# One more gate product by seven, three heads at a time, and weight sums over whole groups, in a gated hybrid transformer block

## The chip, the cores and the metric

One core of one Trainium2 chip runs the kernel in a single launch. Its engines are TensorE (PE, with the weight loads as PEld), VectorE (DVE), ScalarE (ACT), GpSimd (POOL) and SyncE (SP), which issues almost all transfers. The metric is the device time of one execution in microseconds (us), and the median over several executions where there are several. All inputs and the output are float32 in device memory.

## The reference, cut to what matters

One transformer block over 256 tokens of width 2048 (`q`, `k`, `v` heads of 128 columns):

```
h    = rms_norm(x)                                    # 256 x 2048
proj = h @ w_in                                       # 2048 x 11270: q,k,v of 6 + 6 heads, logits, 4 memory heads, 3 gates x 2048
o_fox = softmax(q k^T scale + c_q - c_k, causal) @ v  # 6 heads; c: running sums of log_sigmoid(logits)
log_beta = log_sigmoid(z);  z = q k^T scale           # 6 stick-breaking heads
log_1m   = where(before, log_beta - z, 0)
a        = where(before, exp(log_beta + sum of log_1m over later keys), 0);  o_sb = a @ v
o_mem = softmax(q mk^T scale) @ mv                    # 4 heads; mk, mv = rms_norm(mem) @ w_mem_kv
g     = sigmoid(gates + b_gate)                       # three gates of 256 x 2048
merged = g0*(o_fox @ w_br_fox) + g1*(o_sb @ w_br_sb) + g2*(o_mem @ w_br_mem)
x = x + merged @ w_out                                # 2048 x 2048
u = conv3(rms_norm(x) @ w_up)                         # 2048 x 11264
out = x + (silu(u[:, :5632]) * u[:, 5632:]) @ w_down  # 5632 x 2048
```

## The kernel before

**Three passes.** A weight tile of 128 x 1024 is loaded by SP (`raw`, L140), ACT rounds it to the matmul type (`hi`, L141), DVE subtracts to get the rest (`lo`, L142), and each product is three matmuls: rows of x high with `hi`, low with `hi`, high with `lo` (`passes` L148, `three` L284). `product` (L156) runs a whole product of 256 rows and n columns over pairs of k-tiles, one raw tile per pair, and calls `tick` after each pair. Rings of four tiles each (`WBUFS`, `SBUFS`) hold raw, hi and lo.

**Blocks by eight and by seven.** `blocked` (L324) computes 1024 columns at a time over pairs of k-tiles. A pair has two blocks of rows, two of k and two of columns, so plainly it has 8 block products of three matmuls each (`eight`, L346). A pair "by seven" has 7 products of sums of blocks instead, as in Strassen's scheme in Winograd's form. It needs sums of x (`pair_sums`, L290: five DVE sums, copies on ACT and subtractions) and sums of the weight blocks. After the last seven of a block, four banks `Y` are added into the four results (`gather`, or `gathered` at L963 for the gates). The order of a block's pairs is a string, `e` for an eight, `s` for a seven, `f` for forming the sums of x of one pair (L225 to L227):

```
o_plans = ("eessesse", "eesesese")
g_plans = (("", "", "esesesee"), ("esesesee", "esesesee", "esesesee"))
d_plans = ("ef" * 5 + "ssef" * 4 + "seeee", "efefefesssfe" + "ssse" * 2 + "ssssee")
```

`g_plans[m][b]` is for gate b in columns m x 1024 on, and an empty string means two plain products of 512 columns.

**Where weight sums come from.** For the gates `prepared` (L393, four DVE sums) makes them on the spot, one entry of the plan ahead (`ahead`). For the output product (o) and the down projection (d), they are made long before: `weight_sums` (L243) takes halves of groups of 256 of 512 columns from a queue `halves`, loads the half into a staging tile, makes the sums with three DVE additions (L267 to L269) and stores them in device memory (`kept`, L272). It is a generator that `tick` moves on by one step. `seven` (L369) later loads two raw tiles, two sums T1 and T2, and T3, T4 from there.

**The order of work.** `tick` (L102) moves every generator of `background` on, and up to `WINDOW` = 2 of the queue that `later` fills: heads (`mem_head`, `fox_head`, `sb_head`), transposes (`heads_T`, `merged_T`), gathering. A generator `yield`s where others' work comes between. A stick-breaking head (L871) makes z on PE, log_beta and log_1m on ACT and DVE, two selects on POOL (`diagonal`, L863), splits into `ls` (L890, L891), sums with PE into r (L895), then DVE, ACT's exp, two more selects, and the product with v (`weighted`). `in_order` keeps an instruction at its program place on its engine; the rest is put in order by the scheduler. SP issues its transfers strictly in one order, so a load behind a store waits for that store's data.

**The stages.** kv of the memory, the memory queries (`mq`), the forgetting heads' products f0 to f4 (the last with 262 columns, L780), the stick-breaking ones s0 to s4 (s4 with 256, L913), gates for columns 0 to 1023 (m = 0) with the heads beside them, branches, gates m = 1, branches, output product o (two blocks), up projection (L1159, with convolution and silu beside it), and down projection d (two blocks of 22 pairs, L1225). The sums of x for the gates, `xs` (L840), lie in the slot of the residual `xres`, which is loaded a second time at L1017. Sums of a pair for d lie in `sf` (L1198) or, in the second block, where the pairs of x no longer needed were.

## Time and profile before

| what | value |
| --- | --- |
| runs (three), median | 1467.25 us (1466.77 to 1467.32) |
| profiled execution, its own time | 1466.63 us |
| its span | 1464.9 us |
| PE busy | 1459.6 us, 7335 records |
| PEld / DVE / ACT / POOL busy | 1235.3 / 1192.2 / 839.0 / 21.7 us |
| transfers | 369.55 MB, mean 252 GB/s |
| granted clock, whole span | 1.000 |

A page of the profile is one execution. Busy time sums the time in which an engine had an instruction at work, in us and as a share of the span; matmuls overlap each other, so the mean of one matmul in the groups (394 ns) is more than its share of the time. Names are the program's, and L12 is line 12 of the code above. In a group, `out<-in` names the tiles, x counts instructions, and after the bar stand busy us, the mean ns of one, and idle time ahead with what ended it. A row of waits reads: engine, tile and line that waited, what released it, us in sum, count, longest. A tile name is the program's: `lo_s` belongs to the products s0 to s4, `pre_d` is a staging tile of the weight sums for d.

### The profile page before, as it was taken

The page shows a single profiled execution, that of the slowest core. Times are in us where ns is not written, and L with a number is a line of the kernel's source. Part 1 is how long each engine was busy: PE and PEld are TensorE (multiplying, and loading weights), DVE is VectorE, ACT ScalarE, POOL GpSimd, SP SyncE. Part 2 cuts the span into 40 slices and gives each one's busy share as a digit, 9 for nine tenths or more (in the row PEclk, how much of TensorE's full clock was granted, in tenths as well). Part 3 has the DMA queues.
Part 4 walks back from the last instruction along what each step waited for, and adds up shares of the span by engine and source line. Part 5 has one row for each costly group of instructions (what it writes and reads, how often), then busy time and mean ns, then how long its engine had stood idle before and what let it go on. Part 6 is the DMA issues. An engine that isn't in the chain of part 4 may idle for free.

```text
span 1464.9 us, 20666 instructions
## 1 busy us (share of the span) xinstructions
PE 1459.6 (100%) x7335; PEld 1235.3 (84%) x7335; DVE 1192.2 (81%) x1816; ACT 839.0 (57%) x1194; POOL 21.7 (1%) x48
## 2 busy tenths in 40 slices
PE   9999999999999999999999999999999999999998
PEld 7888888888888888888888888888888888888887
DVE  5777676776588899997877889888888887997887
ACT  6755454464364455546666656556556556674664
POOL 0000000021000000000000000000000000000000
PEclk9999999999999999999999999999999999999999
DMA  9686787687868576778777889888888876798796
GB/s 309 198 281 189 222 279 218 186 265 217 258 190 281 169 222 203 270 260 279 257 194 229 276 281 294 276 282 289 288 285 284 277 235 196 254 319 267 263 333 215
DMA packets 205606, 369.55 MB, mean 252 GB/s; under 512 B 13578, under 2 KB 82078, under 8 KB 205246
## 3 DMA queue, kind: packets, MB, share of 16 engines
q1 hardware_dynamic: 204094, 365.99, 78.3%
q10 hardware_dynamic: 1328, 2.11, 0.4%
q8 instruction: 57, 0.93, 0.2%
q14 instruction: 47, 0.39, 0.1%
q0 software_dynamic: 80, 0.13, 0.0%
HBM read 335.67 MB, written 32.51 MB: 251 GB/s over the span
## 4 chain that ended last, share of the span: by engine, by line
PE 99%; DVE 0%; ACT 0%; POOL 0%; issue 0%; POOLq 0%; DVEq 0%
PE u L1174 22%; PE u L1175 11%; PE xd L288 4%; PE xd L287 4%; PE xd L286 4%; PE xg L286 3%; PE xg L287 3%; PE xg L288 3%; PE f L288 2%; PE f L286 2%; PE f L287 2%; PE s L286 2%; PE s L288 2%; PE s L287 2%; PE g L286 2%; PE b L286 2%
## 5 line engine op out<-in xcount | busy, mean ns | idle before, releaser
L1174 PE MATMUL u<-hT,hi_u 128*128 128x512 f32 x1232 | 428.3, 394 | 0.0
L1175 PE MATMUL u<-hT,lo_u 128*128 128x256 f32 x1232 | 341.4, 277 | 0.0
L1174 PEld LDWEIGHTS u<-hT,hi_u 128*128 128x128 f32 x1232 | 231.0, 188 | 53.6
L142 DVE TENSOR_TENSOR lo_u<-raw_u,hi_u 128x1024 fp32r<-128x1024 f32 x176 | 214.9, 1221 | 63.8 <-ACT hi_u L141 62.9
L141 ACT CAST hi_u<-raw_u 128x1024 fp32r<-128x1024 f32 x176 | 184.8, 1051 | 137.1 <-PE u L1174 120.5
L1175 PEld LDWEIGHTS u<-hT,lo_u 128*128 128x128 f32 x1232 | 231.3, 188 | 0.0
L281 DVE TENSOR_TENSOR lo_d<-raw_d,hi_d 128x1024 fp32r<-128x1024 f32 x88 | 106.8, 1223 | 20.2 <-ACT hi_d L280 17.5
L280 ACT CAST hi_d<-raw_d 128x1024 fp32r<-128x1024 f32 x88 | 91.8, 1053 | 47.6 <-PE xd L287 22.2
L280 ACT CAST hi_g<-raw_g 128x1024 fp32r<-128x1024 f32 (+1 forms) x64 | 61.7, 972 | 37.7 <-PE xg L287 12.4
L281 DVE TENSOR_TENSOR lo_g<-raw_g,hi_g 128x1024 fp32r<-128x1024 f32 (+1 forms) x64 | 70.9, 1117 | 4.3 <-ACT hi_g L280 4.3
L141 ACT CAST hi_f<-raw_f 128x1024 fp32r<-128x1024 f32 (+1 forms) x40 | 38.5, 966 | 52.1 <-PE f L287 47.3
L142 DVE TENSOR_TENSOR lo_f<-raw_f,hi_f 128x1024 fp32r<-128x1024 f32 (+1 forms) x40 | 44.7, 1119 | 27.9 <-ACT hi_f L141 25.9
L287 PE MATMUL xd<-hi_d,aT 128*128 128x512 f32 x170 | 66.2, 389 | 0.0
L286 PE MATMUL xd<-hi_d,aT 128*128 128x512 f32 x170 | 66.2, 389 | 0.0
L288 PE MATMUL xd<-lo_d,aT 128*128 128x512 f32 x170 | 66.2, 389 | 0.0
L142 DVE TENSOR_TENSOR lo_s<-raw_s,hi_s 128x1024 fp32r<-128x1024 f32 (+1 forms) x40 | 44.7, 1117 | 25.2 <-ACT hi_s L141 24.6
L141 ACT CAST hi_s<-raw_s 128x1024 fp32r<-128x1024 f32 (+1 forms) x40 | 38.4, 961 | 43.9 <-PE s L287 27.1
L1174 PE MATMUL u<-hT_rest,hi_u 128*128 128x512 f32 x176 | 62.0, 394 | 0.0
L1125 ACT ACTIVATE y<-u,taps 128x256 f32<-128x256 f32 x88 | 49.6, 596 | 17.0 <-DVE u L1120 16.9
L142 DVE TENSOR_TENSOR lo_g<-raw_g,hi_g 128x1024 fp32r<-128x1024 f32 x32 | 39.3, 1232 | 22.9 <-ACT hi_g L141 22.4
L141 ACT CAST hi_b<-raw_b 128x1024 fp32r<-128x1024 f32 x32 | 33.5, 1052 | 40.5 <-PE b L287 13.5
L141 ACT CAST hi_g<-raw_g 128x1024 fp32r<-128x1024 f32 x32 | 33.6, 1050 | 37.7 <-PE g L287 34.8
(482 smaller groups left out, 3533.7 us busy)
## 6 DMA issues: line engine op xcount, KB each, us to landing
raw_u<-in_w_up_dram SPq DMA_DIRECT2D x176, 512.0 KB, 5.1
raw_g<-in_w_in_dram SPq DMA_DIRECT2D x96, 512.0 KB, 4.3
raw_d<-in_w_down_dram SPq DMA_DIRECT2D x66, 512.0 KB, 5.1
pre_d<-in_w_down_dram SPq DMA_DIRECT2D x88, 256.0 KB, 4.5
kept_d<-pre_d SPq DMA_DIRECT2D x44, 512.0 KB, 6.1
raw_f<-in_w_in_dram SPq DMA_DIRECT2D x32, 512.0 KB, 4.7
raw_s<-in_w_in_dram SPq DMA_DIRECT2D x32, 512.0 KB, 3.8
raw_o<-in_w_out_dram SPq DMA_DIRECT2D x25, 512.0 KB, 5.5
```

Of the source, the lines that this page charges most:

```text
L141: pin(nc.scalar.copy(hi[:, :m], raw[:, :m]))
L142: pin(nc.vector.tensor_tensor(lo[:, :m], raw[:, :m], hi[:, :m].bitcast(F32), ALU.subtract))
L280: nc.scalar.copy(hi[:, :n], src)
L281: nc.vector.tensor_tensor(lo[:, :n], src, hi[:, :n].bitcast(F32), ALU.subtract)
L286: fix(nc.tensor.matmul(o, lhsT=ah, rhs=w[0], start=first, stop=False))
L287: fix(nc.tensor.matmul(o, lhsT=al, rhs=w[0], start=False, stop=False))
L288: fix(nc.tensor.matmul(o, lhsT=ah, rhs=w[1], start=False, stop=last))
L1125: nc.scalar.activation(y, u[:, 2:], AF.Identity, scale=tap(2), bias=tap(3))
L1174: nc.tensor.matmul(ps[i], lhsT=hi[:, j, c], rhs=hT(k + j), start=first, stop=False)
L1175: nc.tensor.matmul(ps[i][:, :S], lhsT=lo[:, j, c], rhs=hT(k + j)[:, :S], start=False, stop=last)
```

## The change

Plans: the second gate of the first 1024 columns gets the string of the others; the second output block has four sevens instead of three; the two blocks of d have 11 and 14 sevens instead of 9 and 13. That is 33 groups with kept sums for o and d instead of 29, and five of the six gate blocks by seven instead of four.

Weight sums: `pair_sums_ahead` takes whole groups (one load of 128 x 2048, three additions, one store), one per six steps during the products f0 to s3, in two staging tiles in the slot of `xres`, the sums three steps and the store five steps after the load. `half_sums` goes on with halves during the gates. In the up projection there is one stream of whole groups in one staging tile `ends`, from step 22 on, one per eight steps.

Heads: the window is three from the queueing of the stick-breaking heads until the first block by seven asks for their end, and two elsewhere. The sums of x for the gates move from the queue into the background of the first gate's product, with junk tiles for scratch.

Down projection: eleven pairs' sums are formed in the first block instead of nine; those of two pairs lie in slots of `rbc`, `taps` and the constants' rows, and in a tile `sf_more`.

The diff, cut to that:

```diff
-WINDOW = 2
 GS = 3
+PF = 6
+DU = 22
...
-        while waiting and len(active) < WINDOW:
+        while waiting and len(active) < window[0]:
...
-    o_plans = ("eessesse", "eesesese")
-    g_plans = (("", "", "esesesee"), ("esesesee", "esesesee", "esesesee"))
-    d_plans = ("ef" * 5 + "ssef" * 4 + "seeee", "efefefesssfe" + "ssse" * 2 + "ssssee")
+    o_plans = ("eessesse", "eessesse")
+    g_plans = (("", "esesesee", "esesesee"), ("esesesee", "esesesee", "esesesee"))
+    d_plans = (
+        "efefefef" + "sef" * 4 + "ssefsfssfssee",
+        "efefef" + "sss" + "esss" * 3 + "ssee",
+    )
...
+    def sums_in(w):
+        both = w[:, 1:2].to_broadcast([P, 2, w.shape[2]])
+        in_order(nc.vector.tensor_tensor(w[:, 0:2], w[:, 0:4:3], both, ALU.add))
+        in_order(nc.vector.tensor_tensor(w[:, T2], w[:, T1], w[:, T2], ALU.add))
+        in_order(nc.vector.tensor_tensor(w[:, T4], w[:, T2], w[:, T4], ALU.add))
...
+    def pair_sums_ahead(staging, period, add, store, end=None, delay=0):
+
+        for _ in range(delay):
+            yield
+        while len(halves) > 1 and halves[0][-1] == 0 and end not in issued:
+            name, wv, nb, pr, _ = halves.popleft()
+            halves.popleft()
+            kept = kept_for(name, nb, pr)
+            w = staging(f"pre_{name}{nb}_{pr}")
+            in_order(
+                nc.sync.dma_start(
+                    w.rearrange("p (k c) -> p k c", k=2), wv[:, 2 * pr : 2 * pr + 2, nb * PIECE : (nb + 1) * PIECE]
+                )
+            )
+            w = w.rearrange("p (i c) -> p i c", i=4)
+            for _ in range(add):
+                yield
+            sums_in(w)
+            for _ in range(store - add):
+                yield
+            in_order(nc.sync.dma_start(kept, w))
+            for _ in range(period - store):
+                yield
...
-    background.append(
-        weight_sums(lambda name: gp.tile([P, 1024], F32, tag="pre", bufs=1, name=name), 6, 4, "merged", slower=2, add=2)
-    )
     finish()
+    staged = cst.tile([P, 2, 2 * PIECE], F32, tag="xres", name="staged")
...
+    background.append(pair_sums_ahead(in_turn, PF, 3, 5, "s3"))
...
-    later(x_sums())
...
+    window[0] = 3
     for h in range(N_SB):
         later(sb_head(h))
 
     ps = proj(C_SB + 1536, 512, "s3")
+    issued.add("s3")
...
+            pair_sums(xT.pair(p), (junk(f"xa_{p}"), junk(f"xr_{p}")), [(xs[:, p], slice(0, 4))])
...
+    background.append(x_sums())
+    background.append(
+        half_sums(lambda name: gp.tile([P, 1024], F32, tag="pre", bufs=1, name=name), 6, 2, 4, "merged")
+    )
...
                     issued.add("heads")
+                    window[0] = 2
...
-    for i in range(2):
-        background.append(
-            weight_sums(
-                lambda name, i=i: ff.tile([P, 1024], F32, tag=f"end{i}", bufs=1, name=name), 8, 6, delay=22 + 2 * i
-            )
-        )
+    ends = []
+    ends_tile = lambda name, dt: ff.tile([P, 2, PIECE], dt, tag="ends", bufs=1, name=name)
+    background.append(
+        pair_sums_ahead(lambda name: ends_tile(name, F32).rearrange("p i c -> p (i c)"), 8, 1, 5, delay=DU)
+    )
...
-    sf = xt_pool.tile([P, N0, 3, 2, P], F32R, tag="xt", name="sf")
+    sf = xt_pool.tile([P, 28, 2, P], F32R, tag="xt", name="sf")
```

Three places in the engines' orders. The first is SP's, from the end of f4 into s0 (`raw_f4_k` and `raw_s0_k` are the weights of pairs from k-tile k on; `pre_o0_3_0` and `kept_o0_2` are a half to be summed and a store of one). Before:

```order
L272 DMA kept_o0_2_1570<-pre_o0_2_1_1710 512x1x256
L140 DMA raw_f4_10_1834<-in_w_in_dram 128x2x262
L258 DMA pre_o0_3_0_1831<-in_w_out_dram 128x2x256 x2
L140 DMA raw_f4_12_1852<-in_w_in_dram 128x2x262
L140 DMA raw_f4_14_1873<-in_w_in_dram 128x2x262
L140 DMA raw_s0_0_1904<-in_w_in_dram 128x2x512
L140 DMA raw_s0_2_1923<-in_w_in_dram 128x2x512
L140 DMA raw_s0_4_1941<-in_w_in_dram 128x2x512
L140 DMA raw_s0_6_1962<-in_w_in_dram 128x2x512
L272 DMA kept_o0_3_1830<-pre_o0_3_0_1831 512x1x256
```

The same place of the changed kernel, where `staged` is the pair of staging tiles:

```order
L141 DMA raw_f4_12_1841<-in_w_in_dram 128x2x262
L302 DMA kept_o1_1_1702<-staged_861 128x2048
L141 DMA raw_f4_14_1859<-in_w_in_dram 128x2x262
L141 DMA raw_s0_0_1892<-in_w_in_dram 128x2x512
L141 DMA raw_s0_2_1910<-in_w_in_dram 128x2x512
L141 DMA raw_s0_4_1929<-in_w_in_dram 128x2x512
L292 DMA staged_861<-in_w_out_dram 128x2x1024
L302 DMA kept_o1_2_1821<-staged_861 128x2048
L141 DMA raw_s0_6_1949<-in_w_in_dram 128x2x512
```

A load of 1 MiB (L292) and a store of 1 MiB (L302) now stand together, ahead of `raw_s0_6`; before, a load of half that size and a store of half that size stood six loads apart.

The second place is POOL's, the selects of the stick-breaking heads (`sb_h` is the block of head h; the first time a head appears it is log_1m's selects, the second time the weights'). Before:

```order
L866 AFFINE_SELECT sb_0_2887<-sb_0_2887 128x128 x2
L866 AFFINE_SELECT sb_1_2898<-sb_1_2898 128x128 x2
L866 AFFINE_SELECT sb_0_2887<-sb_0_2887 128x128 x2
L866 AFFINE_SELECT sb_1_2898<-sb_1_2898 128x128 x2
L866 AFFINE_SELECT sb_2_3120<-sb_2_3120 128x128 x2
```

And in the changed kernel:

```order
L894 AFFINE_SELECT sb_0_2705<-sb_0_2705 128x128 x2
L894 AFFINE_SELECT sb_1_2716<-sb_1_2716 128x128 x2
L894 AFFINE_SELECT sb_2_2745<-sb_2_2745 128x128 x2
L894 AFFINE_SELECT sb_0_2705<-sb_0_2705 128x128 x2
L894 AFFINE_SELECT sb_1_2716<-sb_1_2716 128x128 x2
L894 AFFINE_SELECT sb_2_2745<-sb_2_2745 128x128 x2
```

Three rounds of two heads have become two rounds of three.

The third place is DVE's at the start of the second gate of the first 1024 columns. Before, it is a plain product (`lo_g0_1_k`: columns from 0 on, gate 1, k-tile k), and the last pair of heads is beside it:

```order
L142 TENSOR_TENSOR lo_g0_1_2_3471<-raw_g0_1_2_3469,hi_g0_1_2_3470 128x1024
L891 TENSOR_TENSOR ls_4_3432<-sb_4_3355,ls_4_3432 128x384
L891 TENSOR_TENSOR ls_5_3435<-sb_5_3366,ls_5_3435 128x384
L142 TENSOR_TENSOR lo_g0_1_4_3507<-raw_g0_1_4_3505,hi_g0_1_4_3506 128x1024
L992 SCALAR_TENSOR_TENSOR g_0_0_1_3438<-g1_0_0_3230,scales_111,bg_1_0_3032 128x512
L267 TENSOR_TENSOR pre_d0_1_0_3466<-pre_d0_1_0_3466 128x512
```

In the changed kernel it is the block by seven (`lo_g01_k`), and the sums of its weights (L428 to L431) come between its subtractions:

```order
L311 TENSOR_TENSOR lo_g01_6_3451<-raw_g01_6_3448,hi_g01_6_3450 128x1024
L311 TENSOR_TENSOR lo_g01_7_3469<-raw_g01_7_3466,hi_g01_7_3468 128x1024
L311 TENSOR_TENSOR lo_g01_0_3503<-raw_g01_0_3484,hi_g01_0_3502 128x512
L1040 SCALAR_TENSOR_TENSOR g_0_0_1_3441<-g1_0_0_3264,scales_111,bg_1_0_3005 128x512
L428 TENSOR_TENSOR t0_g01_0_3488<-raw_g01_0_3484 128x512
L429 TENSOR_TENSOR t0_g01_0_3488<-raw_g01_0_3484,raw_g01_1_3486 128x512
L1040 SCALAR_TENSOR_TENSOR g_0_0_1_3441<-g1_0_1_3265,scales_111,bg_1_0_3005 128x512
```

The heads' rows have left this place, and four additions per seven have come to it.

More of the change, by code (lines that the diff above doesn't have):

```diff
@@ L272, in weight_sums @@
             in_order(nc.sync.dma_start(kept[:, :, h * 256 : (h + 1) * 256], w))
-            for _ in range(period - store + (slower if "heads" in issued else 0)):
+            for _ in range(period - store):
[6 more added lines that the diff above has]
+            halves.popleft()
+            kept = kept_for(name, nb, pr)
+            w = staging(f"pre_{name}{nb}_{pr}")
[7 more added lines that the diff above has]
+                yield
+            sums_in(w)
+            for _ in range(store - add):
+                yield
+            in_order(nc.sync.dma_start(kept, w))
+            for _ in range(period - store):
                 yield
@@ L448, in hybrid_block @@
     memres = xt_pool.tile([P, NT, D], F32, tag="xt", name="memres")
+    all_rows = cst.tile([2 * KT + 4, 2, P], F32, tag="rows", name="all_rows")
     def load_rows(q, srcs, name):
-        n = sum(r for _, r in srcs)
-        rows = cst.tile([n, P], F32, name=f"rows_{name}")
+        rows = all_rows[: sum(r for _, r in srcs), 0]
         at_row = 0
@@ L838, in fox_head @@
         weighted(pT, vf, h, h, A)
-    xs = cst.tile([P, GS, 4, 2, P], F32R, tag="xres", name="xs")
-    def x_sums():
-        for p in range(GS):
-            pair_sums(xT.pair(p), block(f"xw_{p}"), [(xs[:, p], slice(0, 4))])
-            yield 2
     later(running_sums())
@@ L1091, in a_pair @@
             return aT[:, 2 * p : 2 * p + 2]
[L1092 to L1094 removed]
+        if not ends:
+            ends.append(ends_tile("a_ends", F32R).rearrange("p i (k c) -> p i k c", k=2))
+        return ends[0][:, p - FA // 2]
     uv = ctx.enter_context(ExitStack())
@@ L1215, in form @@
         formed[0] += 1
-        if p < N0:
-            groups = [(sf[:, p], slice(0, 3))]
+        if p == 9:
+            sf_rest.extend(cst.tile([P, 2, P], F32R, tag=tag, name=f"sf_{tag}") for tag in ("rbc", "taps", "rows"))
+        if p < 9:
+            groups = [(sf[:, 3 * p : 3 * p + 3], slice(0, 3))]
+        elif p == 9:
+            sf_more.append(place([P, 2, 2, P], F32R, "sf", "sf_more"))
+            groups = [(sf_more[0], slice(0, 2)), (sf_rest[2], 2)]
         else:
```

60 lines of the change are left out of this document (36 added, 24 removed).

## The prediction

> **What bounds the kernel now.** I read the page first: the busy shares, then the chain that ended last.
>
> ```profile
> span 1464.9 us, 20666 instructions
> ## 1 busy us (share of the span) xinstructions
> PE 1459.6 (100%) x7335; PEld 1235.3 (84%) x7335; DVE 1192.2 (81%) x1816; ACT 839.0 (57%) x1194; POOL 21.7 (1%) x48
> ...
> PE 99%; DVE 0%; ACT 0%; POOL 0%; issue 0%; POOLq 0%; DVEq 0%
> ```
>
> TensorE is busy all the time, and 99% of the chain is TensorE. A busy PE could still hide short waits, so I asked next what PE waited for.
>
> ```profile
> PE spare L91 <- DVE qscale L487: 1.2, 1, 1.2
> PE r L895 <- DVE ls L891: 0.2, 1, 0.2
> ```
>
> That is the whole list: 1.4 us. So the time is the number of matmuls times their pace, plus a start and a tail. The pace is in the table of windows; the number behind PE's busy time is the count of matmuls.
>
> ```profile
> 1250.00:1450.00 200.00, 200.00 (x884) 165.70 (x883) 170.06 (x223) 128.59 (x160) 0.00 (x0) 1.00 0.86 292
> 405.60:447.10 41.50, 41.50 (x185) 34.38 (x184) 35.08 (x41) 27.11 (x29) 0.00 (x0) 1.00 0.68 217
> 358.00:400.00 42.00, 42.00 (x192) 35.06 (x191) 26.79 (x33) 16.96 (x19) 1.44 (x4) 1.00 0.79 248
> 505.00:615.00 110.00, 110.00 (x486) 90.99 (x486) 100.23 (x120) 62.20 (x65) 0.00 (x0) 1.00 0.69 217
> ```
>
> The columns are: stretch, length, PE, PEld, DVE, ACT, POOL (busy us and count), granted clock, DMA share, GB/s. In the first row 884 matmuls of 512 columns take 200 us: **0.227 us each** (the 389 ns of the groups overlap). The clock is 1.00 throughout. The second row is the third gate of the first 1024 columns, done by seven: 183 matmuls in 41.5 us, the same pace.
>
> **The change, part by part.**
>
> *Matmuls removed.* A pair of k-tiles by eight has 8 x 3 = 24 matmuls, by seven 7 x 3 = 21. The second gate of the first 1024 columns goes from two plain products (192) to five eights and three sevens (183): -9. The second output block gets one more seven: -3. The down projection goes from 9 + 13 = 22 sevens to 11 + 14 = 25: -9. Together 21 x 0.227 = **4.77 us**. Everything else must be asked whether it hides behind PE.
>
> *The second gate by seven.*
>
> ```profile
> L397 DVE TENSOR_TENSOR t_g<-raw_g 128x512 f32<-128x512 f32 x12 | 8.2, 687 | 6.9 <-DMA raw_g<-in_w_in_dram 6.9
> L281 DVE TENSOR_TENSOR lo_g<-raw_g,hi_g 128x1024 fp32r<-128x1024 f32 x52 | 62.8, 1218 | 3.2 <-ACT hi_g L280 3.2
> L281 DVE TENSOR_TENSOR lo_g<-raw_g,hi_g 128x512 fp32r<-128x512 f32 x12 | 8.2, 684 | 1.1 <-ACT hi_g L280 1.1
> ```
>
> DVE pays per seven four sums of 0.687 and parts of 3 x 1.218 + 0.684 = 4.34, against 2.44 for an eight: +4.65. Three of them and the eight gathering operations (about 0.7 each) are +19.6 us; the weight sums in that stretch and the last round of heads go elsewhere. The measured row for the same work is the third gate: DVE 35.1 of 41.5 us. I take that one. The nearest case of such blocks in a row is the 505-615 row: DVE 100.2 of 110 with no wait of PE. Cost 0; if DVE fell behind by what the sum leaves (26.8 + 19.6 - 4 for weight sums = 42.4 against 41.5 us, the heads left in), about 1 us.
>
> *Sums of x moved into the first gate; junk tiles instead of blocks.* Three times about 2.5 us of DVE in a stretch whose DVE has room; PE needs them 60 matmuls later. Cost 0, at most one such set, 2.5 us.
>
> *Three heads at a time.* Rows of the second round now, two heads: the chain of waits for PE, the timeline for POOL and DVE.
>
> ```profile
> 322.39 0.43 PE z L878 x2
> 336.71 0.35 PE r L895 x2
> 346.02 0.43 PE z L725 x2
> 325.64 0.54 POOL L866 TENSOR_SCALAR_AFFINE_SELECT sb<-sb 128x128 f32<-128x128 f32 x2 [10.36 <-PE g L287]
> 326.64 1.52 POOL L866 TENSOR_SCALAR_AFFINE_SELECT sb<-sb 128x128 f32<-128x128 f32 x2 [0.46 <-DVE sb L884]
> 340.05 0.72 POOL L866 TENSOR_SCALAR_AFFINE_SELECT sb<-sb 128x128 f32<-128x128 f32 x2 [0.69 <-ACT sb L899]
> 326.72 1.29 DVE L142 TENSOR_TENSOR lo_g<-raw_g,hi_g 128x1024 fp32r<-128x1024 f32 x1
> 328.74 0.56 DVE L891 TENSOR_TENSOR ls<-sb,ls 128x384 fp32r<-128x384 f32 x1 [0.17 <-ACT ls L890]
> ```
>
> From z (ends 322.8) the last ls is ready at 329.3: 6.5 us, and PE comes to r 13.9 us after z. A third head adds about 2 us of ACT, 1.7 of DVE and one pair of selects, mostly overlapped: 9 to 10 us. The new order keeps 60 matmuls (13.6 us) between z and r in the second round and about 12 us in the first, where some are of 256 columns. From r (337.6) to the last select (340.8) it is 3.2 us of the 8.4 before PE needs it (346.0); the third head adds 0.56 + 0.52 + 2 selects, about 2.3. Cost 0; one round's wait of 0.2 us may go, which is the gain's upper end. If the spare of 2.9 us is used up, see the rivals.
>
> In these rows a select takes 0.27 us alone, and a pair 1.52 us where a DVE subtraction with two inputs lies across it (326.7 to 328.0). [...]
>
> *Weight sums per whole group, ahead of the sums.*
>
> ```profile
> L267 DVE TENSOR_TENSOR pre_d<-pre_d 128x512 f32<-128x512 f32 x44 | 30.0, 682 | 0.0
> L268 DVE TENSOR_TENSOR pre_d<-pre_d 128x256 f32<-128x256 f32 x44 | 18.7, 425 | 1.1
> 70.00:280.00 210.00, 210.00 (x1030) 177.05 (x1030) 149.70 (x265) 103.67 (x166) 4.57 (x12) 1.00 0.76 235
> ```
>
> A half costs DVE 0.68 + 2 x 0.42 = 1.53 us, two halves 3.06; a whole group about 1.22 + 2 x 0.69 = 2.6. In the f and s products (70 to 280 us) twelve whole groups replace twelve halves at the same period of six steps: DVE +12 x 1.1 = 13 us on 150 of 210, hidden. The transfers double: 12 x (1 MiB in, 1 MiB out) instead of half, +12.6 MB on 49.4: **295 GB/s instead of 235**. Bounds from rows: below, 292 GB/s at a share of 0.86 over 200 us (first table), with no wait; above, the rows that follow. I take 0 and keep the burst as a rival.
>
> ```profile
> 176.00:186.00 10.00, 10.00 (x65) 9.11 (x64) 3.81 (x6) 4.42 (x7) 0.00 (x0) 1.00 0.73 206
> 186.00:196.00 10.00, 10.00 (x71) 9.42 (x70) 7.15 (x10) 5.60 (x8) 0.00 (x0) 1.00 0.99 330
> L288 PE MATMUL s<-lo_s,xT x18: 389/390/398, 193.1 to 205.4; 128*128 128x512 f32 x18
> L142 DVE TENSOR_TENSOR lo_s<-raw_s,hi_s x8: 1217/1224/1226, 189.4 to 205.9; 128x1024 fp32r<-128x1024 f32 x8
> DMA to landing us min/median/max: 2.9/3.6/6.1
> ```
>
> In f4 (262 columns) a step is half as long, so the groups come twice as often. Already now the queues are full there (0.99, 330 GB/s), a load takes up to 6.1 us, and DVE is only 2.5 us ahead of PE (190.6 against 193.1). In the new order of SP a group's load and the store of another stand together ahead of raw_s0_6. The store waits for sums that follow the last f4 subtraction; behind it wait raw_s0_6 and all later loads, ACT and DVE wait for these, and PE for them. 2.1 MB at 350 GB/s are 6 us, and the sums about 2.4: the tile comes some 4 us later than now. Loads run four tiles ahead of ACT and DVE four ahead of PE, so I expect about 1 us to spare: 0, with 0 to 3 us kept.
>
> *Up projection.* One group of whole size per eight steps replaces two streams of halves; the bytes are the same, DVE saves 0.4 us per group. The one staging tile waits for the store three steps (8 us) earlier; waits of this kind exist now and PE does not feel them:
>
> ```profile
> SPq L258 <- DMA kept_d<-pre_d: 48.4, 35, 4.7
> ```
>
> Cost 0; the cover is the four-tile lead.
>
> *Down projection.*
>
> ```profile
> 1236.00:1346.00 110.00, 110.00 (x488) 91.14 (x487) 99.98 (x152) 70.18 (x92) 0.00 (x0) 1.00 0.83 277
> 1386.00:1396.00 10.00, 10.00 (x46) 8.29 (x45) 6.53 (x7) 5.59 (x7) 0.00 (x0) 1.00 1.01 361
> 1426.00:1436.00 10.00, 10.00 (x46) 8.29 (x45) 6.54 (x6) 5.58 (x7) 0.00 (x0) 1.00 1.00 371
> L294 DVE TENSOR_TENSOR fw<-aT 128x512 f32<-128x512 f32 x13 | 9.0, 690 | 0.2
> ```
>
> First block, DVE: 100.0 us, plus two sevens (+1.9 each) and two forms (0.69 + 0.42 + 2 x 0.29 + 0.55 + 0.29 = 2.5 each) is 108.8; the first form of the next block and half of the gathering (2.7) move out of it: 103.6 of 108.6 us. Tight, but the forms stand just before their use and the subtractions lead. Transfers: a seven moves 1.84 MB in 4.77 us, 385 GB/s, more than any row shows; at 371 each seven in a run is 0.18 us late, at 350 0.47. The longest run has five where it had four: 0.9 to 2.4 us, against four tiles of lead and the rows above, where four in a row cost nothing. I take 0, with 0 to 2 us kept.
>
> **The sum.** The profiled execution took 1466.63 us (span 1464.9). 1466.63 - 4.77 = 1461.86. The median of the runs shown is 0.62 us above that execution, so the forecast for a median is **1462.5**.
>
> **The rivals.**
>
> *A part is lost* to the burst at f4/s0, to DVE in the first down block or to the five sevens: 2 to 3 us of the ranges above. For it: share 0.99 and 2.5 us of lead; against it: no such wait now. Time about 1465.0.
>
> *The selects become the end of the heads.* If each of six selects stands behind one DVE operation: 6 x (0.27 + 1.22) = 9 us from 338.4, 347.4 against 346.0, 1.4 to 2 us in each of two rounds: about 1466.0. Against it: the pair at 340.05 took 0.72.
>
> *Slower: the DMA queues become the bound of the f and s products.* 62 MB must pass in 210 us plus the lead of about 15 us (four raw and four split tiles): from below 276 GB/s on, PE waits. At 262 it takes 237 us, 12 us too long, and the end is 1462.5 + 12 = 1474.5; the gain is eaten from 269 on. For it: 330 at 0.99 leaves little. Against it: 292 over 200 us at 0.86, mixed with packets no larger than the new ones.
>
> That the matmuls don't go is excluded: PE's order has 21 rows less.
>
> **How the numbers follow.** Forecast 0.67; a part lost 0.17; selects 0.06; slower 0.10. A measurement of this kernel can tell about 0.2% (2.9 us) from no change: faster is below 1464.3, slower above 1470.2. The forecast's cases with up to 1.8 us lost are faster, and some of the part-lost ones: faster 0.70, same 0.20, slower 0.10. The range: down to 1461.0 (the wait at r gone, and the spread of the runs), up to 1466.5, which takes in the lost parts and the selects and leaves out the slower case.
>
> **What would show it.** Right: PE 21 matmuls fewer, its list of waits as short as now, the first two gates 2 us shorter, the down projection 2 us shorter, 295 GB/s before 280 us. Wrong: PE waiting on lo_s near 200 us (burst), on oT or r between 280 and 340 (heads), on lo_d after 1270 (down), or SP waiting long on staged.

## The result

| | us, median (range) | runs |
| --- | --- | --- |
| before | 1466.80 (1466.19 to 1470.32) | 22 |
| after | 1464.64 (1463.19 to 1466.82) | 22 |

The ratio is 0.9984, 95% interval 0.9978 to 0.9990: 2.2 us faster, clear of zero, under half of the 4.77 us that the removed matmuls are worth, and within the 0.2% that the prediction called "same". The profiled execution after, 1466.82 us, is the slowest of its 22 runs, so its losses are larger than those of a usual run. Its page and PE's list of waits:

```profile
span 1465.1 us, 20555 instructions
PE 1457.1 (99%) x7314; PEld 1231.1 (84%) x7314; DVE 1214.0 (83%) x1794; ACT 848.9 (58%) x1212; POOL 17.0 (1%) x48
```

```profile
PE b L318 <- DVE lo_b L143: 1.5, 2, 0.7
PE spare L92 <- DVE qscale L519: 1.2, 1, 1.2
PE s L318 <- DVE lo_s L143: 0.5, 1, 0.5
PE kv L153 <- ACT memT L182: 0.3, 1, 0.3
PE xg L318 <- DVE lo_t_g L311: 0.2, 1, 0.2
```

PE has 21 records fewer. The kernel before waited in this list only for the initial set-up and once for `r`; now there are four more rows, of which the one at `kv` belongs to the start (a second profile of the kernel before has such rows too). The wait at `r` is gone. A wait's row holds only the time that the profile can give to it; the whole loss is read from how long a stage takes. The table gives, from the traces, the time from the first matmul of a stage to the first of the next (s0 begin: its first 61 matmuls' starts; s0 to branches: the rest of s, the heads and the gates m = 0). Stages that took the same time everywhere are left out. The column `before_again` and the last three are experiments below.

| stage, us | before | before_again | after | again | br_free | mended |
| --- | --- | --- | --- | --- | --- | --- |
| span's start to mq | 58.47 | 58.27 | 59.72 | 58.66 | 60.39 | 57.86 |
| s0 begin | 15.05 | 15.05 | 16.26 | 16.06 | 15.39 | 15.05 |
| s0 to branches m = 0 | 239.31 | 239.31 | 236.66 | 236.84 | 236.80 | 236.83 |
| gates m = 1 | 125.39 | 125.36 | 125.87 | 125.65 | 126.03 | 126.21 |
| branches m = 1 | 44.51 | 44.49 | 46.75 | 45.25 | 44.49 | 44.49 |
| output product | 85.04 | 85.04 | 84.36 | 84.36 | 84.36 | 84.36 |
| up projection | 489.95 | 489.95 | 489.95 | 489.95 | 489.98 | 489.95 |
| down, to the last matmul's end | 224.66 | 224.68 | 222.68 | 222.69 | 222.70 | 222.68 |

The gains all came: 2.65 + 0.68 + 1.98 = 5.3 us. In this execution 3.9 us went back in s0 (1.2), in the gates m = 1 (0.5) and in the branches m = 1 (2.2), the start was 1.25 us later, and the time behind the last matmul was 0.3 us longer (4.2 against 3.9). That leaves the span of 1465.1 us, 0.2 more than before.

**The place that was named.** SP's timeline after, at the end of f4 and the beginning of s0 (start, us, operation), and its waits from 180 to 200 us:

```profile
185.10 3.29 SPq L141 DMA_DIRECT2D raw_s<-in_w_in_dram  x3
188.49 0.42 SPq L292 DMA_DIRECT2D staged<-in_w_out_dram  x1
193.09 0.34 SPq L302 DMA_DIRECT2D kept_o<-staged  x1
193.52 4.01 SPq L141 DMA_DIRECT2D raw_s<-in_w_in_dram  x4
```

```profile
SPq L302 <- DVE staged L251: 4.4, 2, 4.2
```

SP stood from 188.9 to 193.1 us at the store L302, whose sums were not made, and raw_s0_6 was issued at 193.5 us, against 188.5 before (1.3 us of that is the later start). The chain of waits shows how that reaches PE:

```profile
193.52 7.68 DMA raw_s<-in_w_in_dram
201.20 0.02 issue
201.23 1.06 ACT hi_s L142
202.31 1.24 DVE lo_s L143
203.55 0.04 issue
203.59 0.50 PE s L318
```

Behind the wait came a transfer of 7.7 us. The two together used up the lead, which is the time by which a weight part is ready before PE uses it.

**The place that was not named.** SP in the branches m = 1, before and then after, with the waits that hold the two gaps:

```profile
609.96 2.61 SPq L140 DMA_DIRECT2D raw_b<-in_w_br_mem_dram  x2
612.62 0.97 SPq L258 DMA_DIRECT2D pre_d<-in_w_down_dram  x2
613.64 0.94 SPq L1019 DMA_DIRECT2D xres_again<-in_x_dram  x2
616.23 6.86 SPq L140 DMA_DIRECT2D raw_b<-in_w_br_sb_dram  x3
```

```profile
610.25 2.16 SPq L141 DMA_DIRECT2D raw_b<-in_w_br_mem_dram  x2
615.18 0.53 SPq L278 DMA_DIRECT2D kept_d<-pre_d  x1
615.76 0.62 SPq L1067 DMA_DIRECT2D xres_again<-in_x_dram  x1
621.13 0.88 SPq L268 DMA_DIRECT2D pre_d<-in_w_down_dram  x2
622.11 1.44 SPq L141 DMA_DIRECT2D raw_b<-in_w_br_sb_dram  x3
```

```profile
SPq L268 <- DMA kept_d<-pre_d: 4.7, 1, 4.7
SPq L278 <- DVE pre_d L251: 2.7, 1, 2.7
```

The kernel before spaces halves by eight steps once the heads are done (`slower=2` in the removed code); the new `half_sums` keeps six. So a store of a half and the next half's load into the same staging tile now meet here, ahead of the weights of the last branch, which are issued 6 us later (622.1 against 616.2). The matmuls on `lo_b`, from first to last start, before and after:

```profile
L288 PE MATMUL b<-lo_b,oT x64: 389/389/398, 617.3 to 661.1; 128*128 128x512 f32 x64
```

```profile
L318 PE MATMUL b<-lo_b,oT x64: 389/389/499, 617.6 to 663.7; 128*128 128x512 f32 x64
```

43.8 us have become 46.1.

### The profile page after: what moved, and what is told of

The parts are those of the page before. It is cut to its first block, busy times and chain, and to the rows that moved or that the text cites. A ratio compares the mean times of both kernels' runs of the same rounds, so it can differ in the third digit from the quotient of the medians.

```text
span 1465.1 us, 20555 instructions
## 1 busy us (share of the span) xinstructions
PE 1457.1 (99%) x7314; PEld 1231.1 (84%) x7314; DVE 1214.0 (83%) x1794; ACT 848.9 (58%) x1212; POOL 17.0 (1%) x48
## 4 chain that ended last, share of the span: by engine, by line
PE 95%; DVE 2%; DMA 2%; issue 1%; ACT 0%; SPq 0%; DVEq 0%; ACTq 0%
PE u L1220 22%; PE u L1221 11%; PE xg L318 4%; PE xg L317 4%; PE xg L316 4%; PE xd L317 3%; PE xd L316 3%; PE xd L318 3%; PE f L316 2%; PE f L317 2%; PE f L318 2%; PE s L318 2%; PE s L316 2%; PE s L317 2%; PE yd L317 2%; PE yd L316 2%
## 5 line engine op out<-in xcount | busy, mean ns | idle before, releaser
L310 ACT CAST hi_g<-raw_g 128x1024 fp32r<-128x1024 f32 (+1 forms) x80 | 77.1, 972 | 48.9 <-PE xg L317 18.6
L311 DVE TENSOR_TENSOR lo_g<-raw_g,hi_g 128x1024 fp32r<-128x1024 f32 (+1 forms) x80 | 88.7, 1120 | 4.2 <-ACT hi_g L310 4.1
L316 PE MATMUL xg<-hi_g,xT 128*128 128x512 f32 x175 | 68.1, 389 | 0.0
L318 PE MATMUL xg<-lo_g,xT 128*128 128x512 f32 x175 | 68.1, 389 | 0.0
L317 PE MATMUL xg<-hi_g,xT 128*128 128x512 f32 x175 | 68.1, 389 | 0.0
L318 PE MATMUL xd<-lo_d,aT 128*128 128x512 f32 x148 | 57.6, 389 | 0.0
L316 PE MATMUL xd<-hi_d,aT 128*128 128x512 f32 x148 | 57.6, 389 | 0.0
```

Of the source, the lines that this page charges most:

```text
L310: nc.scalar.copy(hi[:, :n], src)
L311: nc.vector.tensor_tensor(lo[:, :n], src, hi[:, :n].bitcast(F32), ALU.subtract)
L316: fix(nc.tensor.matmul(o, lhsT=ah, rhs=w[0], start=first, stop=False))
L317: fix(nc.tensor.matmul(o, lhsT=al, rhs=w[0], start=False, stop=False))
L318: fix(nc.tensor.matmul(o, lhsT=ah, rhs=w[1], start=False, stop=last))
```

## The experiments

Ratios are to the kernel before, run on the same chip, with the 95% interval. Edits are to the changed kernel unless said.

**again**: the changed kernel, unedited.

> The changed kernel once more, to tell what belongs to the program from what belongs to one execution. In its first profile PE lost against the kernel before 1.2 us in the start (kv), 1.2 us at the beginning of s0, 0.4 us in the gates m = 1 and 2.2 us in the branches m = 1, together 5.1 us against 4.77 us of matmuls saved. Theory A (two places of SP's order, the store ahead of raw_s0_6 and the load that waits for its staging tile ahead of raw_b2_1_0, cost time each time; the start is chance): the waits on lo_s near 200 us and on lo_b between 617 and 665 us are there again, 0.8 to 2.2 us each place, the start is 0 or 1.2 us later, and the median is 0.9980 to 0.9990 of before. Theory B (all four are chance of one execution): no wait of PE on lo_s or lo_b here, a profiled span near 1460.5 us.

Measured: 1464.08 us (1463.01 to 1466.34), 0.9979 (0.9970 to 0.9988). s0 begin again lost 1.0 us, the branches 0.75, the gates 0.3; the start lost only 0.2. So both SP places recur and their size varies. That is theory A, at smaller numbers than it named in the branches (0.8 to 2.2), and with a ratio just outside its 0.9980 to 0.9990.

**before_again**: the kernel before, unedited.

> The kernel before once more, for a second profile of it. If the start (kv) and the gates m = 1 are chance in both kernels: the first matmuls of mq come between 58 and 60.5 us, the gates m = 1 take 125.4 to 126.1 us, and s0's first five k-tiles (15.05 us) and the branches m = 1 (44.5 us) repeat without a wait of PE. If the branches or s0 lose time here too, the loss there was not the change's.

Measured: 1466.43 us, one run. Every stage but the start repeats within 0.03 us, and the two places do not lose in the kernel before. The start differs by only 0.2 us between its two profiles; it varies from 57.9 to 60.4 us to mq over the changed kernel and its variants. The gates m = 1 are at the low end twice here, and at 125.4 to 126.3 us in the changed kernel and its variants. So neither the start nor the gates are shown to be chance in both kernels.

**s0_half**: in f4 the groups move on only at every second step.

```diff
-            tick()
+            tick(beside=name != "f4" or k % 4 == 2)
```

> The changed kernel with its groups moved on every second step of f4 only (its 262 columns make steps half as long), so that a group's load and the store of another stand 4 loads earlier on SP (ahead of raw_s0_2, with the store of the group two steps older) and not ahead of raw_s0_6. All twelve groups stay. Theory A (SP's wait for the sums of a group, 4.4 us, holds back raw_s0_6 and what follows): no wait of PE on lo_s, s0 begins 1.2 us shorter, the time is about 1.2 us under the changed kernel's, ratio to before 0.9972 to 0.9980. Rival (the queues are simply full there, 2.1 MB more in 20 us): the wait stays, at 0.5 to 1.5 us, perhaps at another tile, ratio 0.9982 to 0.9990.

Measured: 1464.26 us (1463.29 to 1466.22), 0.9980 (0.9971 to 0.9989): no difference from the changed kernel. In its profile the wait on lo_s is gone, and s0 begin is 15.92 us: a group's load and a store, 2 MB, now go out together ahead of raw_s0_2, which then took 8.8 us to land, and PE waited 0.7 us for a head's copy on DVE instead. The branches m = 1 took 47.17 us in this profile. The burst moved; nothing was won.

**br_late**: two steps more between a half's store and the next load in the branches m = 1.

```diff
-            for _ in range(period - store):
+            for _ in range(period - store + (2 if "last" in issued else 0)):
...
         if m == 1:
+            issued.add("last")
             later(merged_sums())
```

> The changed kernel with two steps more between a half's store and the next half's load in the branches m = 1 (the distance that the kernel before has there), so that the load that waits for its staging tile to be stored stands behind two of raw_b2_1_x instead of ahead of them. The bytes are the same. Theory A (SP stood 4.7 us at that load, and the weights of the branches behind it came 6 us late): PE's waits on lo_b go, the branches m = 1 take 44.7 to 45.2 us instead of 46.9, the time is 1.5 to 2 us under the changed kernel's, ratio 0.9968 to 0.9978. Rival 1 (traffic: the reload of x, 2 MB, and the halves fill the queues): the waits stay, ratio 0.9982 to 0.9990. Rival 2 (VectorE is too full there, with the sums for o): the waits stay too, and the subtractions stand behind other VectorE work, not behind ScalarE or a transfer.

Measured: 1463.96 us (1462.24 to 1465.93), 0.9978 (0.9969 to 0.9987). In the profile, which is its fastest run, the branches take 44.49 us without a wait. The median, though, is that of `again`. So one profile speaks for theory A, and the median does not.

**br_free**: no new halves in the branches m = 1; 18 whole groups in the up projection.

```diff
-        half_sums(..., 6, 2, 4, "merged")
+        half_sums(..., 6, 2, 4, "last")
...
-DU = 22
+DU = 14
...
         if m == 1:
+            issued.add("last")
```

> The changed kernel without new halves in the branches m = 1: six halves there in all instead of eight, and 18 whole groups instead of 17 in the up projection, whose first starts at step 14 instead of 22. Theory A and rival 1 both: PE's waits on lo_b go, the branches m = 1 take 44.7 us, the time is 2 us under the changed kernel's, ratio 0.9968 to 0.9975; if the branch with two steps more does not reach that and this one does, the traffic is the cause. Rival 2 (VectorE too full from the sums for o and the branch sums): half of the waits stay, ratio 0.9978 to 0.9985. One more group in the up projection costs nothing by either, since PE waits nowhere there.

Measured: 1462.59 us (1461.70 to 1464.66), 0.9970 (0.9960 to 0.9981), 1.5 us under `again`. `lo_b` and SP's waits in the same window:

```profile
L318 PE MATMUL b<-lo_b,oT x64: 389/389/397, 617.7 to 661.5; 128*128 128x512 f32 x64
```

```profile
SPq L278 <- DVE pre_d L251: 2.7, 1, 2.7
```

43.8 us, as before the change: the wait for the staging tile is gone, the one for sums is still there and hidden. By the rule written down before this run (this edit helps and two steps more do not), the halves' traffic has a part in the loss, and not only the one wait.

**no_gate2**: the second gate as two products, no halves in the branches m = 1.

```diff
-    g_plans = (("", "esesesee", "esesesee"), ...
+    g_plans = (("", "", "esesesee"), ...
...
-        half_sums(..., 6, 2, 4, "merged")
+        half_sums(..., 6, 2, 4, "last")
...
         if m == 1:
+            issued.add("last")
```

> The changed kernel with the second gate of the first 1024 columns as two plain products again, and no new halves in the branches m = 1 (eight halves, all before); heads three at a time as in the change. By the sum of the prediction: PE 9 matmuls more, from s0's end to the branches 2.04 us longer than with the second gate by seven (238.7 instead of 236.7 us), total 2 us over the kernel with the branches mended, near 1464.6, ratio 0.998 to 0.9988. Rival (the heads three at a time are what gained there, and the seven gives nothing net because VectorE or the weight sums on the spot hold it): the stretch stays at 236.7 to 237.3 us.

Measured: 1465.78 us (1463.81 to 1470.35), 0.9991 (0.9982 to 1.0000). s0 to branches 238.59 us, against 236.8 with the seven: 1.8 to 1.9 us, as the nine matmuls say. The rest to the kernel before, 0.7 us, is not the gate's; 0.5 us of it is the stall between two r matmuls, which is gone. The branches again take 44.49 us without halves. The median is 3.2 us above that of br_free, where 2 were expected; in the profile s0 begin took 15.76 us, the rest is not explained.

**win2**: two heads at a time.

```diff
-    window[0] = 3
+    window[0] = 2
```

> The changed kernel with two heads at a time, the plans and the weight sums as changed. In its order the last two heads' r now stands 24 matmuls (5.4 us) ahead of their product with v, where the first seven's end of the heads is asked for. Theory of the prediction (from r to the last select 3.2 us): that fits, and the time is that of the changed kernel within 0.5 us, with the two waits of r of the kernel before (0.2 to 0.4 us) back. Rival (three at a time are needed for the second gate by seven: the third round ends too late): PE waits 3 to 6 us for log or weight tiles of heads 4 and 5 near 365 us, ratio 1.000 to 1.002.

Measured: 1463.96 us (1463.15 to 1466.35), 0.9979 (0.9970 to 0.9988), the changed kernel's time. s0 to branches is 237.21 us, 0.4 to 0.6 us longer than in the two profiles of the change. Three at a time are not what makes the second gate by seven possible. Nor are they what removed the stall at r: the 24 matmuls of r span 3.23 us here, 3.28 in the change and 3.80 before. The 0.4 to 0.6 us lie in the matmuls of s and of the gates; best_late, with three heads, also took 237.12. So no gain of three at a time is shown.

**pf4**: a group every four steps in the f and s products.

```diff
-PF = 6
+PF = 4
...
-    background.append(pair_sums_ahead(in_turn, PF, 3, 5, "s3"))
+    background.append(pair_sums_ahead(in_turn, PF, 2, 3, "s3"))
```

> The changed kernel with a group every four steps of the f and s products instead of six: 18 whole groups instead of twelve there, 12.6 MB more in 210 us (about 350 GB/s instead of 288), and six fewer in the up projection; nothing is left out. By the rival of the prediction that the queues bound these products: 74.5 MB need 331 GB/s, the most seen over 10 us is 330 to 400, so PE waits on lo_f and lo_s, 3 to 12 us in all, ratio 1.000 to 1.007. If the queues have room beyond that (single rows show 400 GB/s) and only the places of store and load matter: under 2 us more than the changed kernel, ratio 0.998 to 0.9995.

Measured: 1469.05 us (1467.35 to 1471.41), 1.0013 (1.0005 to 1.0022), some 5 us over `again`. The table of windows from 70 to 280 us, for the change and for this one (PE, PEld, DVE, ACT, POOL, clock, DMA share, GB/s):

```profile
70.00:280.00 210.00, 209.35 (x1029) 175.90 (x1029) 158.13 (x262) 103.61 (x167) 5.89 (x12) 1.00 0.84 289
```

```profile
70.00:280.00 210.00, 207.84 (x1014) 173.57 (x1013) 166.26 (x274) 101.73 (x163) 5.02 (x12) 1.00 0.92 333
```

PE now waits at lo_s, at raw tiles through ACT and at the heads. The ratio lies in the range that was given for queues that bound these products. But the mean rate alone is not what costs. Up to 176 us, in the f products, PE is never idle at the same rate:

```profile
70.00:176.00 106.00, 106.00 (x495) 88.20 (x494) 88.29 (x141) 51.91 (x79) 0.00 (x0) 1.00 0.92 334
```

From mq to s0 the stage takes 134.29 us against 134.14. The loss begins at s0, whose first 61 matmuls take 19.17 us against 16.1 in `again`, and there SP stood 5.6 and 3.3 us at stores of groups. Some 0.7 us more is lost between s0 and the branches. So the loss of before is larger at the same place; whether the higher rate or the closer stores make it was not separated.

**best**: both places mended: no group moves in f4, halves as in br_free, 19 whole groups in the up projection from step 6 on.

```diff
-            tick()
+            tick(beside=name != "f4")
...
-DU = 22
+DU = 6
```

> The changed kernel with both places of SP's order mended: no group moves on during f4 (eleven whole groups in the f and s products instead of twelve, none with its load and store ahead of raw_s0_6), no new halves in the branches m = 1 (six in all), and 19 whole groups in the up projection from step 6 on. Theory A (the two waits are what the change lost): no wait of PE on lo_s or lo_b, s0 as long as before, branches m = 1 in 44.5 us, the median 4.8 to 5.2 us under before (matmuls 4.77, heads up to 0.5), near 1461.9, ratio 0.9963 to 0.9971. Rival (what is left is chance of the start and of single late transfers, no part of the change): the same median as with the branches mended alone, 1462.6, ratio 0.9968 to 0.9976.

Measured: 1470.16 us (1463.68 to 1475.10), 1.0017 (1.0001 to 1.0032): slower than before, by neither theory. s0 begin 15.05 and the branches 44.49 us, as theory A said, but the up projection took 493.55 us in the profiled run, the third shortest of twelve. What the runs up to 1475 us lose is in no profile. SP in the up projection, and its wait:

```profile
765.05 0.34 SPq L302 DMA_DIRECT2D kept_d<-pre_d  x1
766.71 3.17 SPq L141 DMA_DIRECT2D raw_u<-in_w_up_dram  x2
781.84 0.37 SPq L292 DMA_DIRECT2D pre_d<-in_w_down_dram  x1
782.30 3.30 SPq L141 DMA_DIRECT2D raw_u<-in_w_up_dram  x3
```

```profile
SPq L292 <- DMA kept_d<-pre_d: 14.5, 2, 11.9
```

Here again a load goes into a staging tile whose store has not landed, with weight loads behind it. But that is at most a part of the 3.6 us. About 2 us are lost from 784 to 794 us, and PE's chain there goes back to a weight tile that was issued at 766.7 us, ahead of the group's load, and took 16.1 us to land. Another 1.2 us are lost at 818 us, where a subtraction stood behind the convolution's work on DVE.

**best_late**: the same, with the groups of the up projection from step 22 on, one per seven steps, and the store one step earlier.

```diff
-    background.append(pair_sums_ahead(..., 8, 1, 5, delay=DU))
+    background.append(pair_sums_ahead(..., 7, 1, 4, delay=DU))
```

> The kernel with both places mended once more, but its 19 whole groups of the up projection start at step 22 (about 805 us) instead of step 6, and come one per seven steps instead of eight. In the run before, groups from step 6 on cost 3.6 us in the up projection: about 765 to 782 us every load took 12 to 16 us, and SP then stood 11.9 us at a group's load that waited for the store of the one before. Theory (that collision alone made it slow): the up projection is back at 489.95 us, the median near 1461.9, 4.8 to 5.2 us under before, ratio 0.9963 to 0.9971. Rival 1 (19 groups, 2 more than in the change, are too many for the up projection's queues or VectorE): PE waits there, ratio 0.998 to 1.002. Rival 2 (only the branches mattered; s0 is in the noise): as with the branches mended alone, 0.9970 to 0.9976.

Measured: 1484.32 us (1480.32 to 1485.43), 1.0111 (1.0097 to 1.0125). That is slower than the theory or either rival had it, and it is not the number of groups (see `mended`). The windows from 880 to 960 us, of this kernel and of br_free, and PE's wait:

```profile
880.00:960.00 80.00, 74.18 (x412) 63.79 (x411) 65.27 (x111) 42.65 (x69) 0.00 (x0) 0.98 0.77 275
```

```profile
880.00:960.00 80.00, 80.00 (x463) 70.64 (x462) 69.80 (x119) 49.07 (x77) 0.00 (x0) 1.00 0.86 292
```

```profile
PE u L1222 <- DVE lo_u L143: 9.9, 5, 3.6
```

DVE is less busy than in the good kernel, and yet late. A product of the up projection has eight steps. With a period of eight the sums fall on the same step of each product, and DVE's lead over PE repeats between 3.9 and 6.2 us (`mended`, from 880 us on); with seven they drift through the products, and at some phases they and the convolutions stand together ahead of a subtraction: the lead falls to 0.05 us. Waits account for some 10 of the 20 us. Some 3.4 more, an estimate from the granted clock, are two stretches of 3.41 us with the clock granted at half, one right behind each of the two longest waits (last section; the mean clock is 0.98 from 880 to 960 and from 1040 to 1120 us, and 1.00 in the other rows of 80 us from 800 to 1200 us). In other stretches after waits a pair of matmuls took 350 to 356 ns instead of 347, at a granted clock of 1.00 and without a wait that the profile names. Why stays open.

**best_halves**: as best_late, with all eight halves and the two steps of br_late.

> As the kernel beside it (no group moved in f4, up projection from step 22 on, one per seven steps), but with all eight halves kept, with two steps more between a half's store and the next load in the branches m = 1, so 18 whole groups in the up projection. It moves 2 MB through the queues in these branches that the other doesn't move there. If SP's wait for the staging tile was the cause in the branches: the same median as the other within 0.5 us, branches m = 1 in 44.5 us. If the traffic beside the 2 MB reload of x was: 1 to 2 us more than the other, with PE's waits on lo_b back in the branches m = 1.

Measured: 1484.94 us (1479.85 to 1486.53), 1.0115 (1.0099 to 1.0131); the period of seven drowns the medians. The profile still says something of the branches m = 1: 45.67 us with a wait of 0.9 us on lo_b, against 44.49 in best_late. So moving the load two steps away is no reliable cure: the halves' presence costs, not only that one wait. That is the second time, after br_free, and one profile (br_late) stands against it.

**mended**: best with the rhythm of br_free: groups of the up projection from step 14 on, one per eight steps.

```diff
-DU = 6
+DU = 14
```

> The changed kernel with both places mended and the up projection's groups in their old rhythm: no group moves on in f4 (eleven whole groups in the f and s products), six halves and none of them in the branches m = 1, 19 whole groups in the up projection from step 14 on, one per eight steps. Theory A (the change lost its time at s0 and in the branches m = 1, and what made the last three slow was the step-6 start and the period of seven): up projection 489.95 us, s0's first five k-tiles 15.05 us, branches 44.49 us, median 4.8 to 5.2 us under before, near 1461.9, ratio 0.9963 to 0.9971. Rival 1 (period and start are not what hurt, 19 groups are too many): PE waits in the up projection, ratio over 0.998. Rival 2 (s0's wait doesn't show in a median): as with the branches mended alone, 0.9970 to 0.9976.

Measured: 1462.02 us (1460.99 to 1471.21), 0.9971 (0.9960 to 0.9982), 4.9 us under before (1466.96) and the fastest of all. s0 begin 15.05, branches 44.49, up projection 489.95 us. PE's list of waits:

```profile
PE spare L92 <- DVE qscale L519: 1.2, 1, 1.2
PE xg L318 <- DVE lo_t_g L311: 0.2, 1, 0.2
```

That is theory A in every stage that it named. The ratio fits rival 2 as well: with the branches alone mended (br_free) the median is 0.6 us higher, too little to tell from the spread of the runs, so the worth of s0 is shown by the stage times and not by the median. One of the twelve runs took 1471.21 us, which nothing here explains. 19 whole groups fit; against best only the start differs, against best_late the start, the period and the store's step.

## Why the prediction was right or wrong, point by point

The measured time lies in the range, near the rival "a part is lost" (1465.0), not at the forecast of 1462.5. Of the chances, the larger one (faster, below 1464.3, 0.70) did not come, the 0.20 for "same" did. The forecast is the time of `mended` (1462.02), the kernel in which PE really waits no more than before. That this agrees to half a microsecond is partly luck: there the stretch from s0 to the branches gave 0.5 us more than the matmuls, and the gates m = 1 took 0.8 us more.

- *Matmuls removed, 4.77 us.* Right: output product -0.68 (three matmuls by 0.227), down -1.98 (2.04), and `no_gate2` puts the second gate at 1.8 to 1.9 (nine matmuls, 2.04).
- *The second gate hides behind PE.* Right. DVE 36.6 of 41.6 us where 35.1 of 41.5 was taken from the third gate, no wait:

```profile
363.70:405.30 41.60, 41.60 (x185) 34.46 (x184) 36.62 (x44) 24.98 (x27) 0.00 (x0) 1.00 0.65 201
```

- *Three heads at a time, 0, with 0.2 us of gain as the end.* The term was mis-sized a little, and its cause is open. By no_gate2 the stretch from s0 to the branches gained 0.7 us besides the gate. The list of waits showed 0.2 us for r; the step from one r matmul to the next there was 0.42 us longer than others, and it is gone. But it is gone in win2 too, with two heads at a time. The selects did not become the end: with three heads a pair takes 0.5 to 1.0 us, as in this row beside DVE operations with two inputs, and PE does not wait. The rival's 9 us took 0.27 us for a select alone, and one DVE operation ahead of each. No run shows either: the pair of 0.54 us from 325.64 us of before stood beside DVE operations too (325.44 to 326.58 us), and why the pair from 326.64 us took 1.52 us was not shown.

```profile
325.16 0.87 POOL L894 TENSOR_SCALAR_AFFINE_SELECT sb<-sb 128x128 f32<-128x128 f32 x2 [0.67 <-DVE sb L912]
```

- *Whole groups in the f and s products, 289 GB/s forecast as 295, "I take 0 and keep the burst".* The place and the mechanism were right (a store waiting for its sums ahead of raw_s0_6, 4.2 us), the value taken was not: "about 1 us to spare" was 0.3 to 1.2 us short, since the load behind it took 7.7 us where the longest of before took 6.1. `mended`, without a group moving there, has 15.05 us again.
- *The step that failed: the weight sums' new order was walked only through f, s, up and down.* The halves that remain in the branches m = 1 were given no price. There the change drops the two extra steps, the store and the next load meet, and beside them stands the reload of x. That cost 0.75 to 2.2 us in the two profiles of the change, and 1.5 us of the median by br_free. How much of it is the meeting and how much the traffic of the halves stays open: br_late speaks for the first in its profile, br_free and best_halves for the second. The diff showed the dropped `slower=2`, and the signs of being wrong did not name lo_b.
- *Up projection 0, "the cover is the four-tile lead".* Right for the change (489.95 in both). It holds for its rhythm only: a start at step 6 cost 3.6 us in its profile, and a period of seven, from step 22 on, cost 20.
- *Down projection 0, tight.* Right: DVE 103.3 of 108.6 us (103.6 forecast), and five sevens in a row run without a wait. The second row is a part of them; over other 10 us from 1400 to 1450 us the queues reach 350 to 370 GB/s, no more than the 371 of before:

```profile
1238.20:1346.80 108.60, 108.60 (x481) 89.86 (x480) 103.27 (x161) 74.61 (x101) 0.00 (x0) 1.00 0.87 283
1426.00:1436.00 10.00, 10.00 (x46) 8.26 (x45) 7.55 (x8) 7.54 (x9) 0.00 (x0) 1.00 0.93 325
```

- *Slower by the queues.* Did not happen at 289 GB/s. In pf4, 334 GB/s over 106 us of the f products cost PE nothing either; the rival's rule, that PE waits as soon as the mean rate falls short, was not seen at work in any run.

What stays open: the gates m = 1 take 0 to 0.9 us more in the changed kernel and its variants than in the two profiles of before, `mended` included. Where time is lost, PE mostly waits at a subtraction of weight sums (`lo_t`) in a seven of the second or third gate (after in the third, again in the second, mended in both). What makes it later was not tried.

## What to carry to other kernels

Where one engine issues the transfers in one order, as SP does here, a store that waits for its sums and a load that waits for its staging tile are barriers for all loads behind them: SP stood 4.2 us at the store in s0 and 4.7 us at the load in the branches m = 1, and the weights behind were issued at 193.5 us instead of 188.5, and at 622.1 instead of 616.2. Walk every place where such a pair stands, not only those where the rate rises, and price it as wait plus the longest transfer behind it, against the lead of the consumers. Give side work a period that fits the main loop's steps, or follow the lead through all phases: here the same groups at a period of seven instead of eight, beside products of eight steps, cost 20 us. When a sum of removed work comes out short, compare stage by stage across repeated profiles; here two stages held most of the loss, and mending them gave the forecast time.

## What the runs showed of the hardware that was not expected

The start of the kernel varies by up to 2.5 us over the profiles of the changed kernel and its variants. A part of PE's chain near its first products, after and then `mended` (start, us, what):

```profile
7.26 0.43 PE kv L155
7.68 0.43 PE kv L153
8.11 0.43 PE kv L154
8.54 0.43 PE kv L155
```

```profile
6.35 0.23 PE kv L155
6.58 0.24 PE kv L153
6.82 0.23 PE kv L154
7.05 0.23 PE kv L155
```

A matmul of 512 columns takes 0.43 us at first and 0.23 us from some moment on. The views give the granted clock as 1.00 there, but the trace's clock records begin only at that moment, and the views count what is ahead of the first record as full speed. The first record stands at 9.20 us in after, at 10.97 in br_free, at 5.36 in `mended`, and between 4.5 and 11.0 in the fourteen profiles, while the first product always came at 5.0 to 6.0 us. So the late starts of after and br_free go with a change of pace that came late; what sets its moment, no run shows. A slower pace was also seen after a wait of PE of 3.4 us in best_late: a matmul of 512 columns and one of 256 together took 0.64 us (938.90 to 939.54 us), where they took 0.35 us before the wait (932.72 to 933.07 us), and there the clock is on record. The row of that stretch has it at 0.50:

```profile
937.72:941.13 3.41, 3.25 (x11) 2.96 (x12) 3.41 (x8) 1.01 (x2) 0.00 (x0) 0.50 0.55 153
```

From about 765 to 776 us the queues moved 73 to 143 GB/s in five profiles, where 280 is the mean of the up projection from 820 to 1200 us, and in best loads of 512 KB took 12 to 16 us to land. It coincides with two small transfers of POOL's, a 1 KB one that turns the row scales (10.7 us in best) and a 128 KB one that spreads them over the partitions (7.6 us in best). In the change it lies under the lead; the groups of best, from step 6 on, met it. Whether the small transfers cause it was not tried.
